# A two-layer hybrid decoder trunk on one core: reciprocal square roots by one VectorE multiply-add and a GpSimd power, in place of a bit-level guess and three Newton steps on VectorE

## The chip, the core and the metric

The kernel runs on one core of a Trainium2 chip. The core has five engines with an instruction queue each, which they work through in order: TensorE (PE; PEld is its weight load), VectorE (DVE), ScalarE (ACT), GpSimd (POOL) and SyncE (SP), which here issues the DMAs. An instruction that waits for another engine holds back everything behind it in its own queue. The metric is the device time of the whole program in microseconds, lower is better.

## The reference, cut to what matters

The input x is 1024 positions by 1024 channels; two layers follow each other. Each layer does this:

```
h = rmsnorm(x, norm_mix) * (1 + sc_m) + sh_m          # mod = silu(c) @ ada_w + ada_b
proj = h @ w_in                                       # 2824 columns, split into three groups
A: sliding-window attention, 8 query heads, 2 key heads, q and k with rmsnorm over 64 and partial rotary
B: HGRN2 gated linear recurrence, 4 heads, chunks of 64;  out = rmsnorm(o_b) * silu(bg)
C: gated DeltaNet, 4 heads, chunks of 64, q and k with l2norm over 64;  out = rmsnorm(o_c) * silu(cg)
x = x + gt_m * (concat(A, B, C) @ w_out)
h = rmsnorm(x, norm_ffn) * (1 + sc_f) + sh_f
x = x + gt_f * ((silu(h @ w_gate) * (h @ w_up)) @ w_down)

rmsnorm(x) = x * rsqrt(mean(x * x) + 1e-6) * gain
l2norm(x)  = x * rsqrt(sum(x * x) + 1e-6)
```

Every `rsqrt` above is one value per position (and head), so there are few of them: they are the subject of the change.

## The kernel before

The positions are worked on in two halves of 512 (`HT`), and a half in four blocks of 128 (`NB`). There are dense pieces, which keep TensorE busy with products of 128 x 128 weights and 512 positions, and mixer pieces (`attention`, `hgrn`, `gdn`), which are long chains of small steps over the blocks. Each dense product is done three times on fp32 operands split into a high and a low part: a weight tile is loaded (`wraw`), ScalarE rounds it to `whi` (line 770) and VectorE subtracts to get `wlo` (line 771), and `mm3` issues three matmuls (lines 799 to 801). `Dense.run` keeps three such weight units loaded ahead.

`tile_hybrid` writes out one sequence of dense pieces; the mixers are generators, and at each `mm3` a pace-keeper decides whether to advance them by a step, so that their instructions are woven into the dense work of the same or the next half. This gives the program order. The framework then schedules that program: it decides the order of the instructions in each engine's queue by its own account of what is ready, so the order in a queue is not simply that of the text, and a change in one helper can move instructions on every engine.

`rsqrt(k, out, in_, n, scale, eps)` is called 72 times on 128 partitions and n columns:

- `n_r`, n = 4, 8 times, in `Norm.stat`: the norms over 1024 channels ahead of the input projection and of the FFN. Line 835 then builds a diagonal matrix from it.
- `g_rr`, n = 8, 16 times, in `gdn`: the l2norm of q and k of a block; lines 612 and 614 use it at once.
- `f_r`, n = 4, 32 times, in `Finish.rest`: the norm of a block's output of B or C; line 402 uses it.
- `a_rs`, n = 10, 16 times, in `attention`: the norm of q and k; lines 276 and 280 use it.

All of a call's 11 instructions stand on VectorE: line 55 forms `rs_v` = in * scale + eps, line 56 makes the first guess `rs_y` out of its bits, and lines 59, 60 and 62 are the Newton step, three times. Each reads what the one ahead of it wrote. The users of the result are VectorE instructions too. GpSimd has none of it; its queue holds the masks and constants of the start, and later the elementwise helpers of the mixers (lines 360, 469, 618 and so on) and of the norms (line 850).

Of the kernel before, what the change touches and what calls it, by code (L numbers as in the profile page):

```python
# [9 lines left out]
F32 = mybir.dt.float32  # L10
F32R = mybir.dt.float32r
I32 = mybir.dt.int32
U8 = mybir.dt.uint8
AF = mybir.ActivationFunctionType
ALU = mybir.AluOpType
# [25 lines left out]
def bc(ap, shape):  # L41
    return ap.broadcast_to(tuple(shape))
# [4 lines left out]


def rsqrt(k, out, in_, n, scale, eps):
    V = k.nc.vector  # L50
    sm = k.small
    v = sm.tile([128, 16], F32, name="rs_v", tag="rs")[:, :n]
    y = sm.tile([128, 16], F32, name="rs_y", tag="rs")[:, :n]
    t = sm.tile([128, 16], F32, name="rs_t", tag="rs")[:, :n]
    V.tensor_scalar(out=v, in0=in_, scalar1=scale, scalar2=eps, op0=ALU.mult, op1=ALU.add)
    V.tensor_scalar(out=y.bitcast(I32), in0=v.bitcast(I32), scalar1=-0.5,
                    scalar2=float(0x5F3759DF), op0=ALU.mult, op1=ALU.add)
    for i in range(3):
        V.tensor_tensor(out=t, in0=y, in1=y, op=ALU.mult)
        V.scalar_tensor_tensor(out=t, in0=t, scalar=-0.5, in1=v, op0=ALU.mult, op1=ALU.mult)  # L60
        o = out if i == 2 else y
        V.scalar_tensor_tensor(out=o, in0=t, scalar=1.5, in1=y, op0=ALU.add, op1=ALU.mult)


def build_consts(k, positions):
    nc, tc = k.nc, k.tc
    cp = k.const
    G, V = nc.gpsimd, nc.vector
    t1 = k.mp.tile([128, 1024], F32, name="h_ld")
# [12 lines left out]
    k.ident = k.identr.bitcast(F32)  # L82
    k.ones = cp.tile([128, 128], F32, name="ones")
    G.memset(k.ones, 1.0)
    yield

    def sel(ap, pattern, base, cm):
# [62 lines left out]
    for q in range(4):  # L150
# [9 lines left out]
                    scalar2=None, op0=ALU.is_equal)  # L160
# [3 lines left out]
    for i, f in enumerate(INV_FREQ):  # L164
        G.memset(fr[:, i:i + 1], f)
    V.tensor_tensor(out=ang, in0=bc(posf[:, :, None], (128, 8, 8)),
                    in1=bc(fr[:, None, :], (128, 8, 8)), op=ALU.mult)
    V.tensor_scalar(out=nn, in0=ang, scalar1=1.0 / (2 * math.pi), scalar2=12582912.0,
                    op0=ALU.mult, op1=ALU.add)
# [3 lines left out]
    for _ in range(4):  # L173
        e2 = math.floor(math.log2(rem)) - 7
        v = math.floor(rem / 2.0 ** e2) * 2.0 ** e2
# [64 lines left out]
def attention(k, lc, h, src, r2):  # L240
# [20 lines left out]
    for b in range(NB):  # L261
# [10 lines left out]
        V.tensor_reduce(out=ss, in_=sq, op=ALU.add, axis=AX.X)  # L272
        rs = k.small.tile([128, 10], F32, name="a_rs")
        rsqrt(k, rs, ss, 10, 1.0 / 64, EPS)
        rq = k.small.tile([128, 8], F32, name="a_rq")
        V.tensor_scalar(out=rq, in0=rs[:, 0:8], scalar1=0.125, scalar2=None, op0=ALU.mult)
# [104 lines left out]
class Finish:  # L381
# [15 lines left out]
    def rest(self):  # L397
        k = self.k
        nc = k.nc
        r = k.small.tile([128, 4], F32, name="f_r")  # L400
        rsqrt(k, r, self.ss, 4, 1.0 / 64, EPS)
        nc.vector.tensor_tensor(out=self.sq, in0=self.sq, in1=bc(r[:, :, None], (128, 4, 64)), op=ALU.mult)
        yield 6.0
        pt = self.pt()
        for p in range(2):
            nc.tensor.transpose(pt[:, p, :], self.sq[:, 2 * p:2 * p + 2, :].rearrange("p a b -> p (a b)"), k.ident)
        ot = k.mp.tile([128, 4, 128], F32, name="f_ot", tag="fo")
        if self.swapped:
            for c in range(2):
                nc.scalar.activation(ot[:, 0:2, 64 * c:64 * c + 64], pt[:, :, 64 - 64 * c:128 - 64 * c], AF.Copy)  # L410
        else:
            nc.scalar.activation(ot[:, 0:2, :], pt, AF.Copy)
        nc.sync.dma_start(out=self.mixr[:, self.t0:self.t0 + 2, 128 * self.b:128 * self.b + 128], in_=ot[:, 0:2, :])
        yield 0.0
# [114 lines left out]
def gdn(k, lc, h, src, r4):  # L529
# [64 lines left out]
    for b in range(NB):  # L594
# [14 lines left out]
        V.tensor_reduce(out=ss, in_=sq, op=ALU.add, axis=AX.X)  # L609
        rr = k.small.tile([128, 8], F32, name="g_rr")  # L610
        rsqrt(k, rr, ss, 8, 1.0, 4 * EPS)
        V.tensor_scalar(out=rr[:, 0:4], in0=rr[:, 0:4], scalar1=0.125, scalar2=None, op0=ALU.mult)
        for j in range(2):
# [647 lines left out]
def tile_hybrid(ctx, tc, names, aps, out):  # L1261
# [38 lines left out]
    k.mp = tp(name="mp", bufs=1)  # L1300
    k.tick = Pace()
    bcg = build_consts(k, w["positions"])
    lcs = []

# [256 lines left out]
```

## Time and profile before

| | |
|---|---|
| time, median of 3 runs (lowest, highest) | 2741.18 us (2739.95, 2748.74) |
| time of the profiled execution | 2744.08 us |
| its span from the first instruction to the last | 2742.4 us |
| PE busy in the span | 2616.8 us (95%) |
| DVE busy | 1869.8 us (68%), 4863 instructions |
| ACT busy | 1158.3 us (42%) |
| POOL busy | 377.9 us (14%), 560 instructions |
| granted TensorE clock, mean | 0.99 of full speed |

The profile is of one execution, which took 1.7 us more than its span and 2.9 us more than the median of the runs. A busy share is an average over stages: TensorE is near its limit over most of the span, and what another engine costs shows only where TensorE stands idle for it. Matmuls overlap in the engine, so busy TensorE is not TensorE at its peak.

### The profile page before, as it was taken

Reading aid. Unit: us, or ns where it says so; the run is one execution under the profiler, and the core shown is the slowest. Engines: PE = TensorE matmul, PEld = TensorE weight load, DVE = VectorE, ACT = ScalarE, POOL = GpSimd, SP = SyncE. Lnnn points to the kernel's source line nnn. Section 1 sums busy time; section 2 is a strip of 40 time slices with the busy share of each in tenths; the row PEclk is TensorE's granted clock in tenths of the full one; section 3 lists DMA queues with packets and bytes.
Section 4 is the critical chain, followed back from the end, with each engine's and each line's share of the span. In section 5 each row is a group of like instructions: output and inputs, shape, how many; then the busy total and the mean of one; then the engine's idle time right before and its main releaser. Section 6 shows DMA issues by size and latency. Waiting matters only on the chain.

```text
span 2742.4 us, 42796 instructions
## 1 busy us (share of the span) xinstructions
PE 2616.8 (95%) x15488; PEld 2117.0 (77%) x15488; DVE 1869.8 (68%) x4863; ACT 1158.3 (42%) x2434; POOL 377.9 (14%) x560
## 2 busy tenths in 40 slices
PE   4989898899999999999999999999999999999999
PEld 3887776777777778887877777898787777788887
DVE  7679886777968567567887757637777854544444
ACT  4636573333445444433344444543344544322222
POOL 6132210402101001311011001211110100100000
PEclk9999999999999999999999999999999999999999
DMA  6644336543333355544433335452332224333323
GB/s 234 195 149 132 115 100 205 167 123 91 122 114 101 110 166 160 181 124 135 128 99 105 108 124 178 134 156 74 98 114 88 70 76 154 117 93 95 93 80 108
DMA packets 171956, 343.96 MB, mean 125 GB/s; under 512 B 20832, under 2 KB 80480, under 8 KB 171744
## 3 DMA queue, kind: packets, MB, share of 16 engines
q1 hardware_dynamic: 170880, 341.16, 40.0%
q8 instruction: 122, 2.00, 0.3%
q14 instruction: 90, 0.74, 0.1%
q10 hardware_dynamic: 864, 0.07, 0.0%
HBM read 299.15 MB, written 42.01 MB: 124 GB/s over the span
## 4 chain that ended last, share of the span: by engine, by line
PE 67%; DVE 17%; issue 5%; POOL 4%; ACT 4%; DMA 2%; SPq 0%; POOLq 0%; ACTq 0%; DVEq 0%
PE gu_ps L799 10%; PE gu_ps L800 9%; PE gu_ps L801 9%; PE dn_ps L799 5%; PE dn_ps L800 5%; PE dn_ps L801 5%; DVE wlo L771 3%; PE p_tm L800 2%; PE p_tm L801 2%; PE p_tm L799 2%; PE o_ps L800 2%; PE o_ps L801 2%; PE o_ps L799 2%; POOL n_xn L850 1%; PE pl L484 1%
## 5 line engine op out<-in xcount | busy, mean ns | idle before, releaser
L770 ACT ACTIVATE whi<-wraw 128x1024 fp32r<-128x1024 f32 (+3 forms) x484 | 422.9, 875 | 788.9 <-PE gu_ps L800 240.6
L771 DVE TENSOR_TENSOR wlo<-wraw,whi 128x1024 fp32r<-128x1024 f32 (+3 forms) x484 | 493.3, 1020 | 271.1 <-ACT whi L770 261.3
L799 PE MATMUL gu_ps<-hhi,whi 128*128 128x512 f32 x1408 | 572.4, 407 | 3.4 <-DVE n_xn L848 2.6
L800 PE MATMUL gu_ps<-hlo,whi 128*128 128x512 f32 x1408 | 559.8, 398 | 0.8 <-DVE hlo L852 0.7
L801 PE MATMUL gu_ps<-hhi,wlo 128*128 128x512 f32 x1408 | 560.2, 398 | 0.0
L799 PEld LDWEIGHTS gu_ps<-hhi,whi 128*128 128x128 f32 x1408 | 267.4, 190 | 74.0 <-issue 13.9
L801 PEld LDWEIGHTS gu_ps<-hhi,wlo 128*128 128x128 f32 x1408 | 266.1, 189 | 61.6 <-issue 0.8
L800 PEld LDWEIGHTS gu_ps<-hlo,whi 128*128 128x128 f32 x1408 | 266.6, 189 | 58.1 <-DVE hlo L852 2.8
L799 PE MATMUL dn_ps<-gt,whi 128*128 128x512 f32 x704 | 287.6, 410 | 2.0 <-DVE xt L1061 1.3
L800 PE MATMUL dn_ps<-gt,whi 128*128 128x512 f32 x704 | 278.5, 396 | 0.4 <-DVE gt L1049 0.4
L801 PE MATMUL dn_ps<-gt,wlo 128*128 128x512 f32 x704 | 277.5, 394 | 0.0
L799 PE MATMUL p_tm<-whi,hhi 128*128 128x256 f32 (+1 forms) x896 | 255.7, 286 | 6.7 <-ACT cx L875 3.5
L800 PE MATMUL p_tm<-wlo,hhi 128*128 128x256 f32 (+1 forms) x896 | 256.2, 286 | 5.8 <-DVE wlo L771 5.8
L801 PE MATMUL p_tm<-whi,hlo 128*128 128x256 f32 (+1 forms) x896 | 254.7, 284 | 0.0
L799 PEld LDWEIGHTS p_tm<-whi,hhi 128*128 128x128 f32 x896 | 170.3, 190 | 9.6 <-ACT cx L875 4.3
L800 PEld LDWEIGHTS p_tm<-wlo,hhi 128*128 128x128 f32 x896 | 170.3, 190 | 9.1 <-DVE wlo L771 7.5
L801 PEld LDWEIGHTS p_tm<-whi,hlo 128*128 128x128 f32 x896 | 170.1, 190 | 1.9 <-issue 1.6
L799 PEld LDWEIGHTS dn_ps<-gt,whi 128*128 128x128 f32 x704 | 132.3, 188 | 37.8 <-issue 7.6
L1061 DVE SCALAR_TENSOR_TENSOR xt<-dn_ps,gth,xt 128x512 f32<-128x512 f32 x144 | 107.8, 748 | 77.1 <-PE dn_ps L801 76.7
L801 PEld LDWEIGHTS dn_ps<-gt,wlo 128*128 128x128 f32 x704 | 132.3, 188 | 31.0
L800 PEld LDWEIGHTS dn_ps<-gt,whi 128*128 128x128 f32 x704 | 132.5, 188 | 30.6 <-DVE gt L1049 4.4
L1046 DVE TENSOR_TENSOR g_t<-g_t,gu_ps 128x512 f32<-128x512 f32 x88 | 60.2, 685 | 119.0 <-PE gu_ps L801 118.6
(409 smaller groups left out, 4436.3 us busy)
## 6 DMA issues: line engine op xcount, KB each, us to landing
wraw<-in_w_gate_dram SPq DMA_DIRECT2D x88, 512.0 KB, 3.7
wraw<-in_w_up_dram SPq DMA_DIRECT2D x88, 512.0 KB, 4.0
wraw<-in_ada_w_dram SPq DMA_DIRECT2D x80, 512.0 KB, 3.7
wraw<-in_w_down_dram SPq DMA_DIRECT2D x128, 256.0 KB, 2.7
wraw<-in_w_in_t_dram SPq DMA_DIRECT2D x48, 512.0 KB, 4.0
wraw<-in_w_in_f_dram SPq DMA_DIRECT2D x32, 512.0 KB, 4.0
wraw<-in_w_out_dram SPq DMA_DIRECT2D x32, 512.0 KB, 4.0
wraw<-in_w_down_dram SPq DMA_DIRECT2D x64, 192.0 KB, 2.4
```

What stands on the lines that cost most here:

```text
L484: T.matmul(pl[r][cols, li, p, :], lh, rh, start=True, stop=True)
L770: nc.scalar.activation(hi[:, 0:n], raw[:, 0:n], AF.Copy)
L771: nc.vector.tensor_tensor(out=lo[:, 0:n], in0=raw[:, 0:n], in1=hi[:, 0:n].bitcast(F32), op=ALU.subtract)
L799: T.matmul(out, lh, rh, start=first, stop=False)
L800: T.matmul(out, lh, rl, start=False, stop=False)
L801: T.matmul(out, ll, rh, start=False, stop=last)
L850: nc.gpsimd.tensor_scalar(out=xn, in0=xn, scalar1=acol[:, i:i + 1], scalar2=bcol[:, i:i + 1], op0=ALU.mult, op1=ALU.add)
L1046: V.tensor_tensor(out=t, in0=t, in1=pss[1], op=ALU.mult)
L1061: V.scalar_tensor_tensor(out=x, in0=ps, scalar=k.gth[l][:, m:m + 1], in1=x, op0=ALU.mult, op1=ALU.add)
```

## The change

`rsqrt` keeps the multiply-add (now line 51) on VectorE. The guess and the Newton steps go, and GpSimd raises the result to the power of -0.5, element by element, with a constant tile `mhalf` that is filled with -0.5 at the start. The output tile is now written by GpSimd.

```
 def rsqrt(k, out, in_, n, scale, eps):
-    V = k.nc.vector
-    sm = k.small
-    v = sm.tile([128, 16], F32, name="rs_v", tag="rs")[:, :n]
-    y = sm.tile([128, 16], F32, name="rs_y", tag="rs")[:, :n]
-    t = sm.tile([128, 16], F32, name="rs_t", tag="rs")[:, :n]
-    V.tensor_scalar(out=v, in0=in_, scalar1=scale, scalar2=eps, op0=ALU.mult, op1=ALU.add)
-    V.tensor_scalar(out=y.bitcast(I32), in0=v.bitcast(I32), scalar1=-0.5,
-                    scalar2=float(0x5F3759DF), op0=ALU.mult, op1=ALU.add)
-    for i in range(3):
-        V.tensor_tensor(out=t, in0=y, in1=y, op=ALU.mult)
-        V.scalar_tensor_tensor(out=t, in0=t, scalar=-0.5, in1=v, op0=ALU.mult, op1=ALU.mult)
-        o = out if i == 2 else y
-        V.scalar_tensor_tensor(out=o, in0=t, scalar=1.5, in1=y, op0=ALU.add, op1=ALU.mult)
+    v = k.small.tile([128, 16], F32, name="rs_v", tag="rs")[:, :n]
+    k.nc.vector.tensor_scalar(out=v, in0=in_, scalar1=scale, scalar2=eps, op0=ALU.mult, op1=ALU.add)
+    k.nc.gpsimd.tensor_tensor(out=out, in0=v, in1=k.mhalf[:, :n], op=ALU.pow)
...
     k.ones = cp.tile([128, 128], F32, name="ones")
     G.memset(k.ones, 1.0)
+    k.mhalf = cp.tile([128, 16], F32, name="mhalf")
+    G.memset(k.mhalf, -0.5)
```

Line numbers of the changed kernel are 10 lower than before between the two places, and 8 lower behind the second (614 becomes 606).

The first place is VectorE's queue in the second half's projection of the first layer, where the calls for `g_rr`, `f_r` and `a_rs` come close together (around 251 to 264 us of the trace before). The queue before, from the reduction that feeds `g_rr` on:

```order
L609 TENSOR_REDUCE g_ss<-g_sq 128x8
L616 TENSOR_TENSOR g_RR<-pv,bh 128x256
L55 TENSOR_SCALAR rs_v<-g_ss 128x8
L336 COPY_PREDICATED scr<-amask,psc 128x256
L56 TENSOR_SCALAR rs_y<-rs_v 128x8
L336 COPY_PREDICATED scr<-amask,psc 128x256
L59 TENSOR_TENSOR rs_t<-rs_y 128x8
L55 TENSOR_SCALAR rs_v<-f_ss 128x4
L339 TENSOR_REDUCE a_mx<-scr 128x4
L60 SCALAR_TENSOR_TENSOR rs_t<-rs_t,rs_v 128x8
L1175 SCALAR_TENSOR_TENSOR wraw,mod_90<-wraw,cond 128x1024
L62 SCALAR_TENSOR_TENSOR rs_y<-rs_t,rs_y 128x8
```

Behind these rows 39 more stand ahead of the first user of `a_rs` (line 276), 27 of them of `rsqrt`. The same queue in the changed kernel, from the row behind that reduction on:

```order
L51 TENSOR_SCALAR rs_v<-g_ss 128x8
L51 TENSOR_SCALAR rs_v<-f_ss 128x4
L51 TENSOR_SCALAR rs_v<-a_ss 128x10
L328 COPY_PREDICATED scr<-amask,psc 128x256
L604 TENSOR_SCALAR g_rr<-g_rr 128x4
L394 TENSOR_TENSOR f_sq<-f_sq,f_r 128x256
L606 TENSOR_TENSOR scg<-pa,g_rr 128x256 x2
L615 TENSOR_TENSOR g_qd<-scg,eg 128x256
L328 COPY_PREDICATED scr<-amask,psc 128x256
L268 TENSOR_SCALAR a_rq<-a_rs 128x8
```

The three multiply-adds now stand together, and the users of the three results (lines 604, 394 and 268) follow three, three and seven instructions behind their own. Over all 72 calls, 20 users stand right behind their multiply-add, 23 have one instruction between and 11 have seven or more.

The second place is GpSimd's queue at the same point of the program. Before:

```order
L879 COPY cx<-carry 128x3
L321 MEMSET scr 128x512
L360 AFFINE_SELECT scr<-scr 128x512
L500 COPY scr<-scr 64x256
L618 TENSOR_TENSOR scg<-scg,be 128x256
L621 TENSOR_TENSOR g_kd<-scg,eg 128x256
L619 TENSOR_TENSOR g_RR<-scg,eg 128x256
```

And now, with line 52 the power and `mhalf` the constant:

```order
L313 MEMSET scr 128x512
L352 AFFINE_SELECT scr<-scr 128x512
L52 TENSOR_TENSOR f_r<-rs_v,mhalf 128x4
L871 COPY cx<-carry 128x3
L492 COPY scr<-scr 64x256
L52 TENSOR_TENSOR g_rr<-rs_v,mhalf 128x8
L52 TENSOR_TENSOR f_r<-rs_v,mhalf 128x4
L52 TENSOR_TENSOR a_rs<-rs_v,mhalf 128x10
L610 TENSOR_TENSOR scg<-scg,be 128x256
L613 TENSOR_TENSOR g_kd<-scg,eg 128x256
L611 TENSOR_TENSOR g_RR<-scg,eg 128x256
```

Four powers have come in between, one of them behind the masking of line 352 (360 before), which waits for ScalarE's softmax output. Of the 72 powers, 11 stand right behind such a masking row (lines 352 and 356) and 11 right behind the copy of line 260 (268 before), which waits for a load or for the previous attention block. Rows of GpSimd named ISA, which set it up, are three in both kernels.

## Rows read from the trace of the kernel before

**Rows 1.** The page's first part: busy time of each engine, share of the span.

```profile
PE 2616.8 (95%) x15488; PEld 2117.0 (77%) x15488; DVE 1869.8 (68%) x4863; ACT 1158.3 (42%) x2434; POOL 377.9 (14%) x560
```

**Rows 2.** Windows: stretch, length, busy PE, PEld, DVE, ACT, POOL (instructions), PEclk, DMA.

```profile
70.00:500.00 430.00, 393.28 (x2992) 333.66 (x2991) 340.36 (x1060) 232.32 (x533) 79.62 (x124) 0.97 0.48 152
500.00:2400.00 1900.00, 1853.51 (x10942) 1488.29 (x10942) 1328.67 (x3485) 806.70 (x1735) 256.79 (x336) 0.99 0.39 121
```

**Rows 3.** Waits of PE, 70 to 500 us: us in total, times, longest.

```profile
PE g_px L696 <- DVE scg L692: 6.0, 4, 5.1
PE g_p L666 <- DVE g_qkT L663: 3.7, 2, 2.5
...
PE pk L307 <- DVE a_ks L295: 0.2, 1, 0.2
```

**Rows 4.** Waits of PE, 500 to 2400 us.

```profile
PE g_p L666 <- DVE g_qkT L663: 13.6, 8, 3.5
...
PE g_px L696 <- DVE scr L692: 0.2, 1, 0.2
```

**Rows 5.** Groups of VectorE instructions by line: busy us, mean ns, idle before.

```profile
L60 DVE SCALAR_TENSOR_TENSOR rs_t<-rs_t,rs_v 128x4 f32<-128x4 f32 (+2 forms) x216 | 43.5, 202 | 3.7
L59 DVE TENSOR_TENSOR rs_t<-rs_y 128x4 f32<-128x4 f32 (+2 forms) x216 | 41.9, 194 | 3.3
L62 DVE SCALAR_TENSOR_TENSOR rs_y<-rs_t,rs_y 128x4 f32<-128x4 f32 (+2 forms) x144 | 30.0, 209 | 2.5
L56 DVE TENSOR_SCALAR rs_y<-rs_v 128x4 int32<-128x4 int32 (+2 forms) x72 | 13.4, 186 | 0.9
...
L62 DVE SCALAR_TENSOR_TENSOR n_r<-rs_t,rs_y 128x4 f32<-128x4 f32 x8 | 1.3, 162 | 0.2
```

**Rows 6.** Windows of line 55 alone: VectorE busy (count), then clock and DMA.

```profile
70.00:500.00 430.00, 3.40 (x19) 0.97 0.48 152
500.00:2400.00 1900.00, 8.60 (x52) 0.99 0.39 121
```

**Rows 7.** Timeline of VectorE, 250.5 to 265 us: start us, us, what.

```profile
255.81 0.17 DVE L62 SCALAR_TENSOR_TENSOR rs_y<-rs_t,rs_y 128x8 f32<-128x8 f32 x1
255.89 0.16 DVE L349 TENSOR_TENSOR a_es<-sink,a_nm 128x4 f32<-128x4 f32 x1
256.01 0.17 DVE L59 TENSOR_TENSOR rs_t<-rs_y 128x8 f32<-128x8 f32 x1
256.21 0.17 DVE L60 SCALAR_TENSOR_TENSOR rs_t<-rs_t,rs_v 128x8 f32<-128x8 f32 x1
256.41 0.17 DVE L62 SCALAR_TENSOR_TENSOR g_rr<-rs_t,rs_y 128x8 f32<-128x8 f32 x1
...
256.84 0.75 DVE L614 TENSOR_TENSOR scg<-pa,g_rr 128x256 f32<-128x256 f32 x2
```

**Rows 8.** Timeline of GpSimd, 18 to 265 us.

```profile
20.28 2.34 POOL L1172 TENSOR_TENSOR adag<-adag,cond 128x1024 f32<-128x1024 f32 x1
...
257.74 0.65 POOL L618 TENSOR_TENSOR scg<-scg,be 128x256 f32<-128x256 f32 x1 [12.82 <-DVE scg L614]
```

**Rows 9.** Groups of GpSimd instructions, shapes apart.

```profile
L469 POOL TENSOR_TENSOR scr<-scr 128x128 f32<-128x128 f32 x48 | 25.3, 553 | 166.2 <-ACT scr L456 166.2
L1172 POOL TENSOR_TENSOR adag<-adag,cond 128x1024 f32<-128x1024 f32 x4 | 10.6, 2658 | 2.1 <-DMA adag<-in_ada_w_dram 2.1
...
L215 POOL TENSOR_SCALAR nega<-nega 128x4 f32<-128x4 f32 x2 | 1.0, 518 | 0.0
```

**Rows 10.** Timeline of VectorE, 18 to 30 us: one copy, beside GpSimd's product and without.

```profile
21.12 1.54 DVE L115 COPY cv<-cv 64x64 f32<-64x64 f32 x1
...
24.75 0.18 DVE L115 COPY cv<-cv 64x64 f32<-64x64 f32 x1
```

**Rows 11.** All waits of the span, longest first: one of GpSimd, one of VectorE.

```profile
POOL scr L360 <- ACT scr L359: 431.5, 28, 35.6
...
DVE hlo L852 <- POOL n_xn L850: 30.2, 42, 1.8
```

## The prediction

> **What bounds the kernel now.** I read the busy times first: TensorE is busy for 95% of the span, VectorE for 68%, GpSimd for 14% [rows 1]. So VectorE's work counts only where TensorE stands still for it. The windows tell two stretches apart [rows 2]. From 70 to 500 us, where the mixers of the first half are squeezed in beside the first projections, TensorE is idle for 430 - 393.3 = 36.7 us and VectorE is 79% busy. From 500 to 2400 us TensorE is idle for only 1900 - 1853.5 = 46.5 us, with VectorE at 70%. Then I ask who ended TensorE's idle time. In the early stretch 12 rows of the waits name VectorE, 18.3 us together [rows 3]; in the later one 12 rows, 31.3 us [rows 4]. These 50 us, with the first 70 us aside, are all that a lighter VectorE can give back directly, out of 2742. The reader is to see that the change takes more VectorE time away than this, so that the question is how much of it passes through to TensorE.
>
> **What is removed.** Ten VectorE instructions in each of 72 calls, 720 in all: eight groups, 142.1 us by their own durations, 197 ns each [rows 5]. But durations overlap in VectorE's pipeline, so I look at starts. Where the next instruction does not need the result, it starts 0.08 us later (255.81 to 255.89); where one Newton step feeds the next, 0.20 us later (256.01, 256.21, 256.41) [rows 7]. So the 720 cost VectorE's queue between 720 x 0.08 = 58 us and 720 x 0.20 = 144 us. The Newton steps stand partly among other work and partly alone; I take 0.15 us, 108 us in all, 1.5 us for a call.
>
> **What is added.** 72 powers on GpSimd, 4 to 10 columns each. No power is in the trace, so I bound its duration p. Below: the smallest arithmetic that GpSimd does here, on 4 columns, takes 0.52 us. Above: its longest, a product of 1024 columns, takes 2.66 us [rows 9]. Between the product of 128 columns (0.55 us) and that of 1024 a column costs (2658 - 553) / 896 = 2.35 ns; if a power takes some ten to fifteen passes of that kind over ten columns, that is 0.24 to 0.35 us on top of 0.55. I take **p = 0.9 us**, as it is nearest to the small products; I know of no row that excludes several times as much, and so keep this as a rival.
>
> **The new wait.** The users of the result are VectorE instructions, so VectorE now waits at the head of its queue for GpSimd, with everything behind it: weight splits, evacuations, the other mixer. The path is VectorE to GpSimd, p, and back. A crossing costs about 0.15 us: line 614 ends at 257.59 and GpSimd's line 618 starts at 257.74 [rows 7, 8]; two make 0.3. Against this stands the VectorE work that the new order puts between multiply-add and user: from none (20 of 72) to seven instructions or more (11), and typically one or two. Two instructions like line 614's take 0.75 us [rows 7], so I estimate the median place's cover at 0.7 us. So a call stalls VectorE for 0.9 + 0.3 = 1.2 us where nothing stands between and for 0.5 us at the median place; over the places I take 0.6 us, 43 us in all. For comparison, the one wait of this kind that is there already, for the norm's GpSimd step, ends 42 times with a mean of 30.2 / 42 = 0.72 us [rows 11].
>
> **What hides GpSimd's side.** GpSimd gets 72 x 0.9 = 65 us more on 378 [rows 1]; its queue has room. If a power stands behind an instruction that itself waits, it is late; that is a rival below. At the start a power comes right behind the 2.34 us product that starts at 20.28 [rows 8], between the masks; it can cost the masks its 0.9 us at most, and the call's result comes earlier by about as much. I count nothing for it. The `mhalf` fill is one more small fill at the start, nothing.
>
> **The sum.** VectorE's queue gets 1.5 - 0.6 = 0.9 us lighter with each call. Line 55 tells where the calls are: 19 in the early stretch, 52 in the later one [rows 6], one before. Early: 19 x 0.9 = 17 us. There VectorE ends half of TensorE's idle time (18.3 of 36.7) and is 79% busy, so I let 0.45 of it through: 7.7 us. Later: 52 x 0.9 = 47 us; TensorE is idle there for 2.4% only, the wait at line 666 for `g_qkT` being the main one, so I let a tenth through: 4.7 us. Together 12.4 us. From the profiled execution's 2744.1 us this gives 2731.7; that execution is 2.9 us above the median of the runs, so against the median the forecast is **2729 us**.
>
> With both unknowns at their ends: p = 0.52 lowers the stall to 0.22 us, 16 us in all, and with 0.20 us an instruction 144 - 16 = 128 us of relief are left in place of 65: a gain of 24 us (2717). With 0.08 us an instruction 58 - 43 = 15 us are left: a gain of 3 (2738). With p = 2.66 the stall is 2.36 us, 170 in all, 62 more than is removed; 19/72 of that x 0.45 and the rest x 0.1 is a loss of 12 (2753).
>
> **A rule against it.** While GpSimd's product ran from 20.28 to 22.62, a VectorE copy that otherwise takes 0.18 us took 1.54 us [rows 8, 10]. The Trainium skill, GPSIMD Engine Reference, section Specifications, says that the two engines share their interfaces to SBUF and get in each other's way on some VectorE instructions; by that rule the trace agrees. If a power held VectorE up through its whole length, the cover between multiply-add and user would be worth nothing, and each call would stall VectorE for 1.2 us in place of 0.6: 72 x 0.6 = 43 us less relief, 22 us left of 65, a gain of 4 us (2737). Power needs little data for its work, so I hold the smaller effect to be likelier. The same page, section Engine selection, advises VectorE for elementwise work, with GpSimd about twice as slow on two inputs. By that figure alone, as an estimate, a power would take 2 x 0.2 = 0.4 us and the sum would come out some 6 us lower; the page has no figure for a power.
>
> **Rivals.**
> - *Hidden anyway.* TensorE's idle time stays what it is, since most of it is the latency of the woven chains (reductions, softmax, the recursion at line 686) and not VectorE's load, or the contention above eats the relief. For it: in the later stretch TensorE is 97.6% busy. Against it: VectorE is the engine that ends half of the early waits. Time 2735 to 2743.
> - *The power is slow* (the other side). If GpSimd works through a power element by element, p may be many times what I take. The point from which it decides: a stall of p + 0.3 - 0.7 equals the 1.5 us removed at p = 1.9 us. At p = 6 us each call stalls VectorE by 5.6 us, net 72 x (5.6 - 1.5) = 295 us, of which 78 us fall into the early stretch. With 0.45 there, and 0.2 later, because such stalls outlast the three weight units that are held ready, this is 35 + 43 = 78 us: 2819. For it: the operation is in no row. Against it: all that GpSimd does here on few columns takes well under 1 us.
> - *The power is late, in GpSimd's queue* (also slower). 22 of 72 stand right behind a masking step or a copy that waits for ScalarE, TensorE or a load. GpSimd's waits for the masking step last 431.5 / 28 = 15.4 us on average [rows 11]. If half of the 22 powers are ready early and are held for that long, VectorE loses 11 x 15.4 = 169 us against the relief of 65; net 104 us, 27 us of it early x 0.45 and the rest x 0.1: a loss of 20 us, 2761. It decides from a mean delay of 65 / 22 = 3 us. Against it: the order was made so that the waits come in time, as far as it foresees them.
>
> **Chances.** My forecast 0.43, hidden or eaten up 0.30, slow power 0.17, late in the queue 0.10. What a measurement of this kernel can tell from no change is about 0.3%, 8 us. So faster 0.43, the same 0.30, slower 0.27. The forecast's own range is 2717 to 2738. To leave out no more than 2 in 10, the range must take in the hidden case, the bound at 2753, the late power and half of the slow one: 2710 to 2795.
>
> **What would show it.** Right: the 720 instructions gone and VectorE's busy time near 1870 - 142 = 1730 us; powers of 0.6 to 1.2 us; new waits of VectorE for line 52 of 20 to 70 us in total; the waits for `g_qkT` and the early stretch's idle time shorter by some 8 us. Wrong: powers of several us; waits for line 52 above 110 us; powers that start long after their multiply-add because the row ahead of them on GpSimd waits; or TensorE's idle time unchanged although VectorE has become lighter. The order of every engine's queue changes with the schedule, so a single wait may also come or go for that reason alone.

## The result and the profile after

The changed kernel takes 2761.31 us (median of 5 runs, 2757.87 to 2767.91), the kernel before 2743.37 us on the same chip (2739.95 to 2748.74). The ratio is 1.0064, 95% interval 1.0049 to 1.0079: slower by 0.6%. The forecast was 2729 us and faster; the time lies inside the range (2710 to 2795), on the other side.

The page's busy times after, to set beside [rows 1]:

```profile
PE 2622.0 (95%) x15488; PEld 2118.2 (77%) x15488; DVE 1783.4 (65%) x4143; ACT 1155.4 (42%) x2433; POOL 477.2 (17%) x633
```

The 720 instructions are gone, and VectorE is busy for 86.4 us less, not 142. The groups of [rows 5] add durations, and those overlap in the pipeline, as the prediction said. The span of the profiled execution is 18.4 us longer (2760.8 against 2742.4 us). In it TensorE is idle for 13.2 us more, and busy for 5.2 us more with the same 15488 matmuls, at a mean granted clock of 0.988 against 0.990. GpSimd is busy for 99 us more, not 65. Here are its groups for the power (line 52), with the mean in ns behind the busy time:

```profile
L52 POOL TENSOR_TENSOR f_r<-rs_v,mhalf 128x4 f32<-128x4 f32 x32 | 37.4, 1168 | 235.0 <-DVE rs_v L51 185.5 <-DVE at_d L674 47.7 <-DVE gg L557 1.7
L52 POOL TENSOR_TENSOR a_rs<-rs_v,mhalf 128x10 f32<-128x10 f32 x16 | 32.2, 2013 | 6.7 <-DVE rs_v L51 4.4 <-DVE at_d L674 2.3
L52 POOL TENSOR_TENSOR g_rr<-rs_v,mhalf 128x8 f32<-128x8 f32 x16 | 29.3, 1829 | 128.4 <-DVE rs_v L51 128.2
L52 POOL TENSOR_TENSOR n_r<-rs_v,mhalf 128x4 f32<-128x4 f32 x8 | 10.0, 1250 | 245.3 <-DVE rs_v L51 232.7 <-DVE g_U L676 12.6
```

72 powers last 108.9 us, 1.51 us each; 0.9 was assumed. And VectorE now waits for them, in 58 of 72 calls. The waits of VectorE, in us, times, longest:

```profile
DVE a_rq L268 <- POOL a_rs L52: 25.1, 14, 3.7
DVE f_sq L394 <- POOL f_r L52: 22.3, 23, 3.1
DVE g_rr L604 <- POOL g_rr L52: 21.9, 14, 1.8
DVE n_acc L827 <- POOL n_r L52: 8.2, 7, 2.2
```

That is 77.5 us, 1.08 us a call. So 86 us of work went and 77.5 us of waiting came: VectorE's queue is 9 us lighter, and the program is 18 us slower. The two windows of [rows 2], after:

```profile
70.00:500.00 430.00, 387.40 (x2916) 326.20 (x2915) 316.09 (x861) 225.46 (x525) 106.54 (x141) 0.95 0.46 146
500.00:2400.00 1900.00, 1844.64 (x10935) 1481.97 (x10934) 1258.03 (x2961) 804.68 (x1732) 328.58 (x391) 0.99 0.39 121
```

TensorE's idle time rises from 36.7 to 42.6 us in the early window and from 46.5 to 55.4 us in the later one, with VectorE less busy in both; the early granted clock falls from 0.97 to 0.95. One place shows a stall that reaches TensorE, the first attention block. GpSimd's timeline, then VectorE's, then TensorE's (start, us, what, idle before and releaser):

```profile
212.26 0.81 POOL L260 COPY vring<-scr 128x128 f32<-128x128 f32 x1 [2.96 <-DMA scr<-tm]
215.83 0.29 POOL L260 COPY vring<-scr 128x128 f32<-128x128 f32 x1 [2.76 <-DMA scr<-tm]
216.09 1.96 POOL L52 TENSOR_TENSOR a_rs<-rs_v,mhalf 128x10 f32<-128x10 f32 x1
```

```profile
213.88 0.17 DVE L51 TENSOR_SCALAR rs_v<-a_ss 128x10 f32<-128x10 f32 x1
213.98 0.19 DVE L674 TENSOR_TENSOR at_d<-scg,g_U 128x30 f32<-128x30 f32 x1
214.21 0.19 DVE L676 TENSOR_TENSOR g_U<-g_U,at_d 128x30 f32<-128x30 f32 x1
218.08 0.17 DVE L268 TENSOR_SCALAR a_rq<-a_rs 128x8 f32<-128x8 f32 x1 [3.69 <-POOL a_rs L52]
218.16 0.28 DVE L272 SCALAR_TENSOR_TENSOR scr<-scr,a_rs,gq 128x64 f32<-128x64 f32 x1
218.36 0.18 DVE L674 TENSOR_TENSOR at_d<-scg,g_U 128x27 f32<-128x27 f32 x1
```

```profile
217.00 0.40 PE L793 MATMUL p_fm<-hhi,wlo 128*128 128x512 f32 x1
220.46 0.29 PE L299 MATMUL pk<-identr,a_ks 128*128 128x128 f32 x1 [3.06 <-ACT a_ks L285]
```

The multiply-add is done at 214.05, but GpSimd's queue stands at a copy that waits for a load; the power starts 2.0 us late and lasts 1.96. VectorE stands still for 3.69 us, and with it line 674, which belongs to another mixer and needs nothing from the power. The key tile `a_ks` comes late through ScalarE, and TensorE, which was busy without a gap up to here, waits for 3.06 us. Then its clock falls. Windows of the same kernel (the number behind the five engines is the granted clock):

```profile
205.00:217.00 12.00, 12.00 (x70) 10.38 (x68) 7.39 (x28) 5.83 (x8) 2.51 (x4) 1.00 0.64 201
217.00:221.00 4.00, 0.94 (x5) 0.50 (x4) 2.88 (x15) 1.01 (x3) 1.05 (x1) 1.00 0.34 101
221.00:228.00 7.00, 5.75 (x23) 4.47 (x22) 6.93 (x28) 4.18 (x9) 2.66 (x6) 0.52 0.29 95
```

The clock is full (2.4 GHz) up to the gap, and behind it come 7 us at 0.52, which is nearly all at the lower of the two levels (1.2 GHz). As an estimate, at full clock the same work would have taken up to 7 x 0.48 = 3.4 us less, on top of the gap of 3 us.

### The profile page after: what moved, and what is told of

It reads as the page before. It is cut to its first block, busy times and chain, and to the rows that moved or that the text cites. A ratio compares the mean times of both kernels' runs of the same rounds, so it can differ in the third digit from the quotient of the medians.

```text
span 2760.8 us, 42153 instructions
## 1 busy us (share of the span) xinstructions
PE 2622.0 (95%) x15488; PEld 2118.2 (77%) x15488; DVE 1783.4 (65%) x4143; ACT 1155.4 (42%) x2433; POOL 477.2 (17%) x633
```

## The experiments

Theory 1: VectorE's waits for a step that is too long give back what the removal won. Theory 2, its rival: the new order of the queues costs the time, whatever the step lasts. The table has every run; waits are those of VectorE for GpSimd at the four places. The ratio is that to runs of before on the same chip, whose median was 2741.7 to 2744.6 us in the five groups; so times of different groups compare to some 3 us.

| kernel | us, median | ratio, 95% interval | VectorE busy | waits | GpSimd busy |
|---|---|---|---|---|---|
| before | 2743.4 | | 1869.8 | 0 | 377.9 |
| changed | 2761.3 | 1.0064 (1.0049, 1.0079) | 1783.4 | 77.5 | 477.2 |
| gp_mult | 2716.7 | 0.9910 (0.9897, 0.9922) | 1781.1 | 12.8 | 393.8 |
| no_power | 2714.7 | 0.9899 (0.9885, 0.9913) | 1777.7 | 0 | 377.0 |
| two_powers | 2841.0 | 1.0356 (1.0339, 1.0373) | 1786.5 | 161.3 | 573.9 |
| vring_act | 2764.2 | 1.0076 (1.0062, 1.0090) | 1782.6 | 74.3 | 471.2 |
| only_a | 2760.7 | 1.0063 (1.0050, 1.0075) | 1844.3 | 28.1 | 410.9 |
| only_g | 2748.5 | 1.0025 (1.0015, 1.0035) | 1851.8 | 22.9 | 392.7 |
| only_f | 2745.8 | 1.0012 (0.9999, 1.0024) | 1830.7 | 23.3 | 417.0 |
| solid | 2724.5 | 0.9930 (0.9915, 0.9944) | 1830.9 | 6.6 | 398.8 |
| idle_power | 2737.7 | 0.9990 (0.9981, 0.9999) | 1781.0 | 42.3 | 504.8 |
| many_mults | 2731.1 | 0.9956 (0.9944, 0.9968) | 1783.2 | 24.0 | 498.0 |
| newton2 | 2720.8 | 0.9925 (0.9914, 0.9937) | 1839.3 | 0 | 376.2 |
| f_all_gp | 2741.4 | 0.9997 (0.9989, 1.0006) | 1825.4 | 0 | 441.3 |
| idle_clean | 2737.2 | 0.9978 (0.9969, 0.9988) | 1782.2 | 23.2 | 500.5 |
| chain_mults | 2767.9 | 1.0104 (1.0083, 1.0124) | 1780.6 | 81.4 | 483.8 |
| newton1 | 2714.9 | 0.9900 (0.9887, 0.9914) | 1812.5 | 0 | 373.6 |
| newton4 | 2753.3 | 1.0037 (1.0023, 1.0051) | 1895.0 | 0 | 374.7 |
| idle_short | 2719.2 | 0.9915 (0.9901, 0.9928) | 1780.5 | 13.0 | 407.4 |
| newton2_idle | 2728.0 | 0.9937 (0.9924, 0.9950) | 1839.3 | 0 | 486.4 |

**The power's length against the order of the queues.**

```
-    k.nc.vector.tensor_scalar(out=v, in0=in_, scalar1=scale, scalar2=eps, op0=ALU.mult, op1=ALU.add)
-    k.nc.gpsimd.tensor_tensor(out=out, in0=v, in1=k.mhalf[:, :n], op=ALU.pow)
+    k.nc.vector.tensor_scalar(out=v, in0=in_, scalar1=0.0, scalar2=-0.2, op0=ALU.mult, op1=ALU.add)
+    k.nc.gpsimd.tensor_tensor(out=out, in0=v, in1=k.mhalf[:, :n], op=ALU.mult)
```

The multiply-add gives the constant -0.2 here and the product 0.1: the root is left out.

> The power on GpSimd is replaced by a multiply of the same tiles there, and the root is left out (the result is the constant 0.1). The instructions stand in the same order on VectorE, GpSimd and TensorE as in the changed kernel; only the length of the step on GpSimd differs. Theory 1 (VectorE's stalls on a power of 1.0 to 2.0 us give back what the removed instructions gained): the 72 steps fall from 109 us to 10 to 30 us, VectorE's waits for them from 77 us to under 35 us, and the kernel is at 2700 to 2740 us. Theory 2 (the new order of the work around the four places costs the time, whatever the step on GpSimd lasts): 2750 to 2765 us.

2716.7 us. The groups of this kernel on GpSimd for three of the four places, and VectorE's waits for all four:

```profile
L52 POOL TENSOR_TENSOR f_r<-rs_v,mhalf 128x4 f32<-128x4 f32 x32 | 11.5, 359 | 237.6 <-DVE rs_v L51 188.1 <-DVE at_d L674 47.7 <-DVE gg L557 1.7
L52 POOL TENSOR_TENSOR g_rr<-rs_v,mhalf 128x8 f32<-128x8 f32 x16 | 6.3, 391 | 132.2 <-DVE rs_v L51 132.0
L52 POOL TENSOR_TENSOR a_rs<-rs_v,mhalf 128x10 f32<-128x10 f32 x16 | 4.3, 266 | 8.1 <-DVE rs_v L51 4.9 <-DVE at_d L674 3.1
```

```profile
DVE f_sq L394 <- POOL f_r L52: 5.6, 11, 2.3
DVE a_rq L268 <- POOL a_rs L52: 2.9, 5, 1.1
DVE n_acc L827 <- POOL n_r L52: 2.3, 4, 1.3
DVE g_rr L604 <- POOL g_rr L52: 2.0, 7, 0.3
```

Every row of VectorE's, GpSimd's and ScalarE's queue stands where it stands in the changed kernel, and TensorE's too but for a few neighbouring matmuls, so theory 2 falls. The length of the step alone is worth 44.6 us by the medians (42 by the ratios), for 64.7 us more of VectorE's waits: 0.69 us per us (0.65). This rate holds everything that the longer step does, in GpSimd's own queue too. Between the two profiled executions lie 47.6 us: in 34.8 TensorE is idle, and for 12.8 it is busy longer with the same matmuls (2622.0 against 2609.2 us), at a mean granted clock of 0.988 against 0.991.

**The relief alone.** The multiply-add writes a constant into the result, and nothing else is left:

```
+    k.nc.vector.tensor_scalar(out=out, in0=in_, scalar1=0.0, scalar2=0.1, op0=ALU.mult, op1=ALU.add)
```

> The multiply-add writes straight into the result and there is no step on GpSimd (the root is left out, the result is the constant 0.1): the relief alone. Theory 1: no wait for GpSimd is left at the four places and the kernel is at 2690 to 2730 us, no slower than the run with a multiply on GpSimd. Theory 2: removing the instructions is worth little by itself and the order is again another one: 2735 to 2765 us.

2714.7 us. All 720 instructions are worth 27 us by the medians of this group; the crossing to GpSimd and back with a short step costs 2 us, within what two runs differ by.

**Twice the power.**

```
+    d = k.small.tile([128, 16], F32, name="rs_d", tag="rsd")[:, :n]
+    k.nc.gpsimd.tensor_tensor(out=d, in0=v, in1=k.mhalf[:, :n], op=ALU.pow)
     k.nc.gpsimd.tensor_tensor(out=out, in0=v, in1=k.mhalf[:, :n], op=ALU.pow)
```

> A second power, whose result nobody reads, ahead of each real one: GpSimd's 72 steps last 109 us more, and VectorE's work is the same. Theory 1: VectorE's waits at the four places rise from 77 us to 150 to 185 us and the kernel is at 2785 to 2850 us. Theory 2: the waits rise as much, but they lie where TensorE doesn't wait for VectorE, and the kernel stays at 2755 to 2775 us.

2841.0 us. VectorE's waits:

```profile
DVE a_rq L270 <- POOL a_rs L54: 55.8, 16, 4.9
DVE f_sq L396 <- POOL f_r L54: 45.3, 24, 4.0
DVE g_rr L606 <- POOL g_rr L54: 44.8, 15, 3.4
DVE n_acc L829 <- POOL n_r L54: 15.4, 8, 3.1
```

83.8 us more of waits, 79.7 us more of time: 0.95 per us, almost all of it by now.

**The copy ahead of the power.**

```
-        G.tensor_copy(k.vring[:, cur, :], at[:, 640:768])
+        A.activation(k.vring[:, cur, :], at[:, 640:768], AF.Copy)
```

> The changed kernel with the copy into the ring of values of line 260 on ScalarE rather than GpSimd, so that the power of the attention block no longer stands behind a copy that waits for a DMA. Theory 1 with the late start as a main part of it: VectorE's wait at a_rq falls from 25 us to 18 to 21 us and the kernel gains 4 to 15 us, 2746 to 2757 us. Theory 1 with the power's own length as the main part: 2756 to 2763 us. Theory 2: no change, 2757 to 2765 us.

2764.2 us. The wait at `a_rq` falls from 25.1 to 22.9 us only and nothing is gained. At the first attention block VectorE's wait falls from 3.69 to 1.96 us and TensorE's from 3.06 to 1.45 us, and yet the program is no faster. What stands at 212 to 218 us above is a real stall, but the copy is not the cause of the loss.

**The power at one place only.** The Newton steps of before stand at the other places, as here for `a_rs`:

```
-        rsqrt(k, rs, ss, 10, 1.0 / 64, EPS)
+        power(k, rs, ss, 10, 1.0 / 64, EPS)
```

> The power only for a_rs (16 calls, 10 columns), the Newton steps for the other 56. Theory 1, with the cost shared out by VectorE's waits: relief 16/72 of the 27 us that the run without a power gained, so -6 us; waits of 22 us beyond the short step's, at the 0.7 us per us that the step from the short to the real power cost (44 us for 65 us), so +16 us: 2748 to 2756 us. Rival 1b, the loss sits at one place, the first attention block near 216 us, and is that of a_rs alone: 2754 to 2763 us. Rival 1c, the calls' loss lies in g_rr and f_r: 2734 to 2742 us.

2760.7 us: as slow as the whole change, out of 16 calls. It is the value of rival 1b, but not its place: the dense product that stands at 326.9 us before stands 2.7 us earlier here, and the lasting loss comes behind it. From 350 to 375 us, only_a:

```profile
350.00:375.00 25.00, 24.14 (x172) 20.27 (x172) 17.98 (x91) 14.98 (x38) 5.56 (x8) 0.77 0.20 65
```

The granted clock is 0.77 there, and 1.00 before.

> The power only for g_rr (16 calls, 8 columns). Theory 1, shared out by the waits: -6 us of relief, 20 us of waits beyond the short step's x 0.7 = +14 us: 2746 to 2754 us. Rival 1b: 2734 to 2742 us. Rival 1c: 2750 to 2758 us.

> The power only for f_r (32 calls, 4 columns, the shortest power). Theory 1, shared out by the waits: -12 us of relief, 17 us of waits beyond the short step's x 0.7 = +12 us: 2737 to 2746 us. Rival 1b: 2728 to 2736 us, since the relief is kept. Rival 1c: 2746 to 2754 us.

2748.5 and 2745.8 us. With 10, 8 and 4 columns the loss is 0.63%, 0.25% and not to be told from nothing. For `g_rr` and `f_r` theory 1 fits; for `a_rs` it is too low by 5 us or more. The net loss grows with the power's length, but `f_r` has twice as many calls and so twice the relief. With a relief of 27 us shared out by calls (6, 6 and 12 us, an estimate), the waits of 28.1, 22.9 and 23.3 us cost about 0.8, 0.5 and 0.6 us per us: no single price, and none that follows the length.

**The same length as work of VectorE.** gp_mult, with a reduction on VectorE between multiply-add and multiply:

```
+    R = {4: 100, 8: 120, 10: 107}[n]
+    k.nc.vector.tensor_reduce(out=w, in_=bc(v[:, :, None], (128, n, R)), op=ALU.max, axis=AX.X)
```

> The run with the short multiply on GpSimd, and in each call a VectorE reduction of 400 to 1070 columns ahead of it that lasts about as long as VectorE waits for the real power (0.5 to 1.3 us, 55 to 65 us in all); the root is left out. It asks whether it is VectorE's lost time that costs, or something else in the wait for GpSimd. If VectorE's time in one piece at these places is what costs: 2750 to 2765 us, as with the power. If a wait costs more than the same time of work (GpSimd's own queue, or what stands behind the power there): 2725 to 2740 us.

2724.5 us. The reductions, as groups:

```profile
L54 DVE TENSOR_REDUCE rs_w<-rs_v 128x4 f32<-128x400 f32 x40 | 22.6, 566 | 0.7
L54 DVE TENSOR_REDUCE rs_w<-rs_v 128x10 f32<-128x1070 f32 x16 | 20.2, 1262 | 0.5
L54 DVE TENSOR_REDUCE rs_w<-rs_v 128x8 f32<-128x960 f32 x16 | 18.4, 1148 | 0.2
```

Against gp_mult, 61.2 us of reductions, by which VectorE is busy for 49.8 us longer, cost 7.8 us by the medians (5 to 6 by the ratios): 0.13 to 0.16 per us, where 64.7 us of waits cost 44.6. This is against theory 1 as first put: VectorE's lost time has not one price. It is no comparison in one order, though. The order takes the reduction into account: the users of `a_rs` stand 9.7 rows behind their multiply-add on average here, 2.0 in the changed kernel. So theory 3 came up: GpSimd's time itself costs.

**GpSimd's time without VectorE's wait.** First with an unread power behind the short multiply:

```
     k.nc.gpsimd.tensor_tensor(out=out, in0=v, in1=k.mhalf[:, :n], op=ALU.mult)
+    d = k.small.tile([128, 16], F32, name="rs_d", tag="rsd")[:, :n]
+    k.nc.gpsimd.tensor_tensor(out=d, in0=out, in1=k.mhalf[:, :n], op=ALU.pow)
```

> The run with the short multiply on GpSimd (the root is left out), and behind each multiply a power of its result that nobody reads: GpSimd does the 72 powers, but VectorE waits for the short multiply only. Theory 1 (VectorE's unplanned waits at the head of its queue cost): VectorE's waits at the four places stay under 35 us and the kernel is at 2716 to 2730 us. Theory 3 (new, since the run with planned VectorE work of the same length cost only 8 us: it is GpSimd's time that costs, by its own queue or by what a power does to the other engines while it runs): 2742 to 2762 us.

2737.7 us, between the two: VectorE still waits 25 us for the unread power at `g_rr`, which it overwrites in place. This decides nothing. With four to eight more short multiplies:

```
+    for i in range({4: 4, 8: 7, 10: 8}[n]):
+        k.nc.gpsimd.tensor_tensor(out=d, in0=v, in1=k.mhalf[:, :n], op=ALU.mult)
```

> The run with the short multiply, and 4, 7 or 8 more multiplies of the same kind ahead of it (for 4, 8 and 10 columns; the root is left out), so that GpSimd is busy for about as long as with a power, without a power, and the order of the queues is nearly that of the changed kernel. If the multiplies last 0.2 us each one behind the other, the step takes 1.0 to 1.8 us. Theory 1, and theory 3 as far as it is GpSimd's queue: 2745 to 2765 us. If it is the power itself that disturbs the other engines: 2716 to 2730 us.

2731.1 us, between the two again. The order put most of these multiplies behind the one that counts, so the waits are 24 us only, and this run is a second form of the one before. Two cleaner runs followed, with the power reading `rs_v`, and the same rows with a short multiply in the power's place:

```
+    k.nc.gpsimd.tensor_tensor(out=d, in0=v, in1=k.mhalf[:, :n], op=ALU.pow)     # idle_clean
+    k.nc.gpsimd.tensor_tensor(out=d, in0=v, in1=k.mhalf[:, :n], op=ALU.mult)    # idle_short
```

> As the run with the short multiply (by a tile of ones, the root left out), and behind each multiply a power of rs_v, whose result nobody reads and which shares nothing with VectorE's later writes at these places but the ring of rs_v: GpSimd does the 72 powers, VectorE waits for the short step only. The order of the queues is that of the changed kernel but for the added rows. If unforeseen waits of VectorE are what costs: VectorE's waits at the four places under 30 us, and 2716 to 2730 us. If GpSimd's time costs: 2738 to 2755 us with waits under 30 us.

> idle_clean with the unread power replaced by an unread short multiply; the order of all four queues is the same, row for row (the root is left out). If the 20 us of idle_clean are GpSimd's time: 2714 to 2724 us. If they come from the order that moved: 2733 to 2741 us.

2737.2 and 2719.2 us, in the same order row for row. The first lies between its two ranges, the second in that for GpSimd's time. The page of idle_clean, and then that of idle_short:

```profile
PE 2619.7 (96%) x15488; PEld 2118.5 (77%) x15488; DVE 1782.2 (65%) x4143; ACT 1153.7 (42%) x2433; POOL 500.5 (18%) x705
```

```profile
PE 2608.8 (96%) x15488; PEld 2112.4 (78%) x15488; DVE 1780.5 (66%) x4143; ACT 1153.5 (42%) x2433; POOL 407.4 (15%) x705
```

93 us of GpSimd's time cost 18 us. VectorE's and ScalarE's busy times are the same within 2 us, so a running power does not slow their instructions; that it acts by its place in GpSimd's queue is what is left, and is argued. TensorE is busy for 10.9 us longer with the same matmuls, at a mean granted clock of 0.988 against 0.992, so more than half of the 18.9 us between the two profiled executions is not idle time. A part of the rest can be seen: the short step of one call stands behind the unread power of another, and VectorE's waits are 10.2 us longer, 8.6 of them for `a_rs`:

```profile
DVE a_rq L270 <- POOL a_rs L52: 11.6, 12, 2.9
```

```profile
DVE a_rq L270 <- POOL a_rs L52: 3.0, 8, 0.8
```

The first row is idle_clean, the second idle_short.

**A chain of the same length without a power.**

```
+    for i in range({4: 4, 8: 7, 10: 8}[n]):
+        k.nc.gpsimd.tensor_tensor(out=d, in0=v, in1=k.ones[:, :n], op=ALU.mult)
+        v = d
```

> The short multiply as a chain of 5, 8 or 9 multiplies on GpSimd (4, 8, 10 columns), each reading the one ahead of it, so that the result is late by about as much as with the power (0.2 us each by their durations: 1.0 to 1.8 us), but the schedule can see that: between multiply-add and user stand 4.4 VectorE rows for a_rs (changed kernel: 2.0) and 2.0 for g_rr (1.0). The root is left out. If the price is that of unforeseen waits: waits at the four places of 25 to 50 us and 2724 to 2745 us. If GpSimd's time costs whatever is foreseen: 2748 to 2765 us.

2767.9 us, slower than both ranges, with waits of 81.4 us: a little worse than with the power, so nothing in the power itself is needed but its length. The order is not the same here: the users of `a_rs` stand 4.4 rows behind their multiply-add on average, in place of 2.0. The hope that this distance would be enough was wrong; the waits did not shrink.

**VectorE's work, step by step.** The range in the loop of before is 2, 1 or 4 in place of 3.

> The kernel before with two Newton steps in place of three: 216 of the 720 instructions gone, no new wait. The run without a power gained 27 us with all 720, so 216/720 of it: 8 us, 2731 to 2739 us. If the chain's own length counts as well as VectorE's time, up to 12 us.

> One Newton step in place of three (432 instructions fewer; the roots are good to about 0.2% only). If VectorE's work has a price that rises with its amount, most is won already with two steps: 2714 to 2721 us. If the price is even and two steps had a lucky order: 2722 to 2732 us.

> Four Newton steps in place of three (216 instructions more). If the price rises with the amount (22 us for the third step, 6 us for the first two and the guess together): 2760 to 2785 us. If it is even at 27/720 us an instruction: 2748 to 2756 us.

2720.8, 2714.9 and 2753.3 us. From no root at all to four steps the times are 2714.7, 2714.9, 2720.8, 2743 and 2753.3: nothing, 6, 22 and 11 us. The first two steps are almost free, the third costs most. newton2 gains about twice what was expected; newton4 lies in the range of an even price and not in that of a rising one, so a price that rises with the amount is not shown. Whether the knee is as sharp as this is open, since each count has an order of its own. The kernel with two steps is a version that beats both: 0.9925 of before (0.9914 to 0.9937). One step is 6 us faster still, but its roots are good to some 0.2% only. The windows of newton2:

```profile
70.00:500.00 430.00, 399.50 (x3071) 340.24 (x3069) 340.05 (x1012) 231.32 (x534) 90.22 (x129) 0.98 0.49 155
500.00:2400.00 1900.00, 1865.32 (x10969) 1497.45 (x10970) 1308.39 (x3333) 808.68 (x1740) 244.48 (x331) 1.00 0.39 121
```

TensorE's idle time is 30.5 and 34.7 us, against 36.7 and 46.5 [rows 2].

**Both together, and GpSimd taking the user too.**

```
+    k.nc.gpsimd.tensor_tensor(out=d, in0=v, in1=k.mhalf[:, :n], op=ALU.pow)     # behind two Newton steps
```

> The kernel with two Newton steps on VectorE, and in each call a power of rs_v on GpSimd that nobody reads (109 us of GpSimd's time); the results are those of the two steps. If GpSimd's time costs by itself, about as much as in idle_clean: 2721 + 15 to 25 = 2736 to 2746 us. If not: 2716 to 2727 us.

2728.0 us: 7 us more than newton2 by the medians, 5 us more against the before of each group, and the intervals overlap. 110 us of GpSimd's time with no wait of VectorE for it are worth a few us here, against 18 in idle_clean; why the two differ is not shown.

With the power for `f_r` alone, GpSimd also takes the product that uses it:

```
-        nc.vector.tensor_tensor(out=self.sq, in0=self.sq, in1=bc(r[:, :, None], (128, 4, 64)), op=ALU.mult)
+        nc.gpsimd.tensor_tensor(out=self.sq, in0=self.sq, in1=bc(r[:, :, None], (128, 4, 64)), op=ALU.mult)
```

> The power for f_r alone, and the product with it (128x256, 0.42 us on VectorE) moved to GpSimd too, right behind the power in its queue, so that VectorE waits for neither; the Newton steps for the other 40 calls. Theory 1: VectorE loses 32 x 10 Newton instructions and 13 us of products, and has no wait: a gain of 10 to 20 us against before, 2724 to 2734 us. Theory 3: GpSimd's 37 us of powers and about 20 us of products cost as much as is gained: 2740 to 2750 us.

2741.4 us, no gain, although VectorE has 44 us less to do than before. TensorE now waits for GpSimd itself:

```profile
PE gf_pt L414 <- POOL f_sq L410: 4.8, 3, 1.9
PE hf_pt L414 <- POOL f_sq L410: 4.2, 4, 1.6
```

The wait has moved from VectorE to TensorE. Read across between newton1 (1812.5 us of VectorE's busy time) and newton2 (1839.3), 1825 us would be at about 2718 us; 9 of the 24 us above that stand in these two rows; the others are not accounted for.

## Why the prediction was wrong

**What bounds the kernel.** The runs agree with the reading: no run that only lightens VectorE goes below 2714.7 us, a gain of 27 us, and the estimate was that about 50 us of waits [rows 3, 4] could be given back at most.

**What is removed.** 1.5 us a call, 108 us, was a little too much: VectorE's busy time fell by 86 us (92 without any GpSimd step), and the idle gaps ahead of the 720 instructions, 12.0 us over the eight groups of [rows 5], went with them. Let through as predicted, 19 x 1.5 x 0.45 + 52 x 1.5 x 0.1 = 21 us; measured 27. This term was nearly right.

**What is added.** p = 0.9 us was mis-sized: 1.01 us for 4 columns, 1.64 for 8 and 1.96 for 10 by the medians, so about 0.38 us plus 0.16 us for each column, where 2.35 ns were read off [rows 9] and multiplied by ten to fifteen. The upper bound of 2.66 us held for the means. The estimate of 0.4 us, worked out with the Trainium skill, GPSIMD Engine Reference, section Engine selection, was too low by a factor of 2.5 to 5; that section names add, multiply and max, and no power.

**The new wait.** 0.6 us a call and 43 us were mis-sized too: 1.08 us and 77.5 us. The error of p accounts for it: 0.6 + (1.51 - 0.9) = 1.2 us a call, so the wait itself was seen rightly. With the measured sizes, and the prediction's own rates of pass-through, 86 - 77.5 = 9 us of relief are left (21 with the small gaps), 9 x (19 x 0.45 + 52 x 0.1) / 72 = 2 us of gain (4): no change. So the sizes explain why the gain was gone, and not why there was a loss.

**The step that failed** is the one that priced a stall like the work removed, as one net figure for VectorE's queue times 0.45 or 0.1, 0.19 on average. 92 us of removed work gave 27 us, 0.29 per us. The waits, with all that the longer step does besides, cost 0.69 per us, and 0.95 further up, while the reductions cost 0.13 to 0.16. The sum also had no term for TensorE's clock: of the 18.4 us between the two profiled executions, 5.2 are matmuls that last longer. In VectorE's busy time and waits together the changed kernel stands at 1783.4 + 77.5 = 1861 us, between newton2 (1839) and before (1870). Read across between these two it would be at 2736 us; it is at 2761. What is shown of the 25 us: a step of the same length without a power costs about as much (chain_mults); GpSimd's time alone accounts for a few us (newton2_idle); where a step that counts can stand behind another call's power, GpSimd's time accounts for up to 18 us, with waits 10 us longer and matmuls 10.9 us longer (idle_clean against idle_short). The rest, it is argued and not shown, is that a wait stands right where the result is needed, while the Newton chain of before was spread: [rows 7] show other rows between its steps. Shown is that the framework orders the power and a short multiply alike, so its order makes no room for the longer step; that a version ordered with the right length would be cheap is argued from solid, and chain_mults, with more distance and no gain, speaks against it.

**What hides GpSimd's side** was wrong in its argument: 14% busy is no sign that a queue has room at the moment that counts. `a_rs` started 2.0 us late at 216 us. Over the 72 calls a power starts 0.44 us behind the end of its multiply-add on average, 31.7 us in all, and 15.0 of these belong to the 25 powers that stand right behind another power.

**The rivals.** The slow power came closest. Its point, p = 1.9 us, is passed by `a_rs` alone; the mean of 1.51 would not have decided it, since the price was set too low. The late power is not the cause: it was to decide from a mean delay of 3 us, and the mean is 0.44. The 11 powers behind a masking step are 1.6 us late in all, and vring_act shows that the 11 copies are not what costs. Hidden anyway is excluded by no_power. The rule of the Trainium skill, GPSIMD Engine Reference, section Specifications, by which the two engines get in each other's way, was weighed as a hold-up through the power's whole length: by that rule VectorE's busy time would grow with GpSimd's 93 us, and the measurement (1782.2 against 1780.5 us) differs, for this operation on few columns. The other way round the trace agrees: long VectorE instructions with two inputs held 10 of the 72 powers back, by 9 us in all, so there the work between multiply-add and user covered little. The last section has the rows.

**The signs named beforehand.** Busy time near 1730 us: 1783. Powers of 0.6 to 1.2 us: right for 4 columns only. Waits of 20 to 70 us were to be right and above 110 wrong; 77.5 lies between, and already meant a loss. TensorE's waits for `g_qkT` did fall, from 17.3 to 15.1 us, but the early stretch's idle time rose by 6 us, where it was to fall by some 8.

## What to carry to other kernels

When work moves off an in-order engine whose next row needs the result, set the time removed against the wait that replaces it, and price the wait higher: in this kernel about 0.7 us per us, with all that the longer step does besides, against 0.1 to 0.3 for work that the schedule can lay among other work. And ask what a gap does to TensorE's clock: here a quarter to more than half of a difference in time stood in matmuls that lasted longer, not in idle time. Measure a step of unknown length by a cheap stand-in in the same order (here the multiply), before counting on it. And look first for less work in place: one Newton step less gave most of what could be won, with no new wait.

## What the runs showed of the hardware

- A power on GpSimd takes about 0.38 us plus 0.16 us for each column of 128 partitions, against 0.20 to 0.21 us (medians) for a multiply of 4 to 10 columns.
- Ten of the 72 powers, and nine of the 72 multiplies of gp_mult, last 0.8 to 1.0 us longer than the others of their kind. Each of them starts while VectorE works on two inputs of 1024 columns for 1.22 us (lines 763 and 1167), every step that starts so is among them, and each such multiply ends 0.06 to 0.07 us behind that instruction. Three more in each kernel are 0.4 us longer, beside such instructions on 512 columns. So a long VectorE instruction with two inputs holds GpSimd's step back until it ends. One case in gp_mult and one in the changed kernel:

```profile
642.40 1.22 DVE L763 TENSOR_TENSOR wlo<-wraw,whi 128x1024 fp32r<-128x1024 f32 x1
642.53 1.14 POOL L52 TENSOR_TENSOR f_r<-rs_v,mhalf 128x4 f32<-128x4 f32 x1 [9.83 <-DVE at_d L674]
```

```profile
659.41 1.22 DVE L763 TENSOR_TENSOR wlo<-wraw,whi 128x1024 fp32r<-128x1024 f32 x1
659.55 1.95 POOL L52 TENSOR_TENSOR f_r<-rs_v,mhalf 128x4 f32<-128x4 f32 x1 [9.83 <-DVE at_d L674]
```

- GpSimd's power does not lengthen VectorE's instructions measurably: 200 products and sums that start while an unread power of idle_clean runs last no longer than the same ones in idle_short (90.1 against 96.3 us). Its 1024-column product, though, stood beside a copy of 1.54 us that otherwise takes 0.18 [rows 8, 10].
